# Group norm statistics of a retention head moved from VectorE to ScalarE, and a state waited for by name

## The chip, the cores and the metric

The kernel runs on one core of a Trainium2 chip. The metric is the device time of one execution in microseconds (us). A core has five engines that run side by side, each through its own queue in order: TensorE (PE in the profile; its weight loads are PEld), VectorE (DVE), ScalarE (ACT), GpSimd (POOL) and SyncE (SP), which here issues all DMAs. They wait for each other through semaphores.

## What is computed

Two layers of a mixer over 1024 rows of width 1024, and a final RMSNorm. In each layer the normalised and modulated rows are projected to 4096 columns; half of them feed four retention heads of width 128, half eight stick-breaking heads of width 64; both halves are gated and projected back. The change lies in the retention, at its end:

```python
def retention(q, k, v):
    ...
    o_inner = jnp.einsum('bhncm,bhnme->bhnce', scores, vc)
    ...
    def step(state, kv_i):
        return state * chunk_dec[None, :, None, None] + kv_i, state
    ...
    o_cross = jnp.einsum('bhncd,nbhde->bhnce', qc, prev) * q_dec[None, :, None, :, None]
    o = (o_inner + o_cross).reshape(b, h, s, v.shape[-1])
    mu = jnp.mean(o, axis=-1, keepdims=True)
    var = jnp.mean(jnp.square(o - mu), axis=-1, keepdims=True)
    return (o - mu) * lax.rsqrt(var + EPS)
```

and then `y_ret = merge_heads(y_ret) * jax.nn.silu(rg)`.

## The kernel before

**Work.** Float32 values are split into two float16 parts (high and low), and each product is three float16 matmuls (high by high, high by low, low by high). Weights come as 128x512 pieces (`wst`), are split on ScalarE and VectorE into `w`, and the normalised rows lie transposed in `hh` and `hl`. A layer runs its four pairs of stick-breaking heads (`stick_project`, then `attend`, `head_pair`, `head_block`, `weigh`: tiles `z`, `beta`, `keep`, `ta`, `av`) and its four retention heads (`retention_project`, `retain`) in an order given by a table, and ends with `out_project`.

**A retention block.** A head has 8 blocks of 128 rows, so that there are 64 blocks in two layers. `retention_project` makes 24 matmuls of 128x512 into `acc` (query, key, value, gate), and starts `retain` for the block. That rotates query and key (`t1`, `t2`, VectorE and GpSimd), splits them, transposes them by DMA into `qkT`, makes the key-value product `pkv` for the state (`rst`, its float16 parts `rs16`; not for the last block), the scores (`psc`), masks and splits them, and adds the products of query by old state and of scores by values in `po`. Then come the statistics: BN_STATS and BN_AGGR on VectorE give mean and variance (`rbs`, `rmv`), GpSimd adds the epsilon column (`rve`) and takes the power -1/2 (`rrs`), VectorE makes `y0` = (po - mean) x gate, and ScalarE and VectorE scale `y0` by `rrs` into the two parts of `yt`. Two blocks' `yt` are transposed by one DMA into `y`, which only `out_project` reads. Up to three blocks are under way at once; `po`, `psc`, `z` and others share five PSUM banks.

**What sets the order.** Nobody writes the order of instructions out. Each piece of work is a generator (a stream) that yields what it needs next: tiles, names marked as done, room in a pool. A planner (`Flow`) keeps a clock for each engine, gives every recorded operation a price, and goes on with the stream of the best rank that is ready by its estimate, TensorE's clock leading, with a slack of 400 on streams that come back to TensorE. The order so found is the order of each engine's queue. A changed price therefore moves work everywhere. At the start, the planner also orders the loads, squares and transposes of the input (`xt`), and the column sums of the first layer's modulation (`sums` from the weights `ada`, 16 matmuls of one column a group).

All recorded operations go through one helper, so that the trace shows them all at line 90; they are told apart by their tiles.

Of the kernel before, what the change touches and what calls it, by code (L numbers as in the profile page):

```python
# [13 lines left out]
F32 = mybir.dt.float32  # L14
AF = mybir.ActivationFunctionType
ALU = mybir.AluOpType
PSUM = bass.MemoryType.PSUM
DRAM = bass.MemoryType.DRAM

P = 128  # L20
# [6 lines left out]
EPS = 1e-6  # L27
# [5 lines left out]
DS = 1.0 / WS  # L33
AS = 256.0
VS = 16.0
RS = 2.0 ** -10


def retention_constants():
    f = np.float32  # L40
    lg = np.log1p(-(f(2.0) ** (f(-5.0) - np.arange(4, dtype=f)))).astype(f)
    i = np.arange(P, dtype=f)
    m, c = i[:, None], i[None, :]
    same = (i[:, None] // 64) == (i[None, :] // 64)
    later = (c // 64) > (m // 64)
    mask = np.zeros((P, 4, P), f)
    qdec = np.exp((i[:, None] + f(1.0)) * lg[None, :]).astype(np.float64)
    for h in range(4):
        dec = np.exp((np.abs(c - m) - (c + 1)).astype(np.float64) * lg[h])
        mask[:, h] = np.where(same | later, dec * np.exp((m - 127.0) * lg[h]), 0.0) * RS  # L50
    kdec = np.exp((f(127.0) - i)[:, None] * lg[None, :]).astype(f)
    bdec = [float(np.exp(f(P) * lg[h])) for h in range(4)]


    cols = np.concatenate([kdec * f(DS * VS), EPS * P * (VS * RS / qdec) ** 2], 1).astype(f)
    return mask, cols, bdec


# [9 lines left out]


MASK, COLS, BDEC = retention_constants()  # L70


# [27 lines left out]
class Flow:  # L100
# [32 lines left out]
    def price(self, kind, name, outs, ins):  # L133
        n = outs[0].free_size()
        if kind == "pe":
            if name == "transpose":
                return 109 if ins[0].dtype == F32 else 64
            if ins[0].dtype == F32:
                return 210 if n < 16 else 61 + n * 4 / 2.4
            rows, cols = ins[0].shape[0], outs[0].shape[0]  # L140
            turn = 97 * (self.shape not in (None, (rows, cols)))
            self.shape = rows, cols
            if 64 in (rows, cols):
                return turn + max(1.5 + n / 4.8, 27)
            return turn + max(2.5 + n / 2.4, 56)
        if kind == "act":
            scales = sum(1 for a in ins[1:] if a.free_size() == 1)
            return n / 1.2 + (51 if ins[0].space == PSUM else 93) + 93 * scales
        if kind == "dve":
            n = max([n] + [a.free_size() for a in ins])  # L150
            if name == "tensor_tensor_scan":
                return 68 + 2.083 * n
            if name == "bn_stats":
                return 170 + n / 0.96
            if name == "bn_aggr":
                return 217
            scales = sum(1 for a in ins if a.free_size() == 1)
            return (n + 65) / 0.96 + 62 * scales
        if kind == "pool":
            if name == "memset":  # L160
                return 36 + 0.84 * n
            if name == "tensor_scalar" and n > 1:
                return 200 + 0.9 * n
            if n == 1:
                return 500 if outs[0].tensor.name.startswith(("rrs", "rs", "r_")) else 268
            return 20 + 3.1 * n if n < 512 else 150 + 2.1 * n
        if name == "dma_start_transpose":
            return 225 + 0.88 * n
        size = outs[0].free_nbytes() * outs[0].shape[0]
        run = 4 * outs[0].shape[-1]  # L170
        return size / run * (8 + 0.037 * run) / 16
# [121 lines left out]
def trunk(ctx: ExitStack, tc, x, c, norm_g, w_ada, b_ada, w_in, w_out, final_g,  # L293
          rot, rmask, rcols, out):
    nc = tc.nc
    flow = Flow()
    pe, act, dve, pool, sp = (Engine(flow, k, e) for k, e in (
        ("pe", nc.tensor), ("act", nc.scalar), ("dve", nc.vector), ("pool", nc.gpsimd), ("dma", nc.sync)))
# [3 lines left out]
    wk = Slots(flow, ctx.enter_context(tc.tile_pool(name="wk", bufs=2)), 2)  # L302
# [16 lines left out]
    def bank(name, tag="g", bufs=5):  # L319
        return ps.tile([P, 512], F32, tag=tag, bufs=bufs, name=name)  # L320
# [40 lines left out]
    rcols_sb = const.tile([P, 8], F32, name="rcols_sb")  # L361
# [605 lines left out]
    def retain(l, h, b, acc, state, turn, mask):  # L967
# [3 lines left out]
        gs = wk.tile([P, P], F32, tag="rg", bufs=3, name="rg")  # L971
        act.activation(gs, acc[:, 384:512], AF.Sigmoid, scale=DS)
        kdec = rcols_sb[:, h:h + 1]
# [8 lines left out]
        roomrot.n += 1  # L982
        dve.scalar_tensor_tensor(out=vd[:, 1], in0=acc[:, 256:384], scalar=kdec, in1=vd[:, 0],
                                 op0=ALU.mult, op1=ALU.subtract)
        dve.scalar_tensor_tensor(out=gs, in0=acc[:, 384:512], scalar=DS, in1=gs,
                                 op0=ALU.mult, op1=ALU.mult)
        pool.tensor_tensor(out=t1[:, 0::2], in0=t1[:, 0::2], in1=t2[:, 1::2], op=ALU.subtract)
        pool.tensor_tensor(out=t1[:, 1::2], in0=t1[:, 1::2], in1=t2[:, 0::2], op=ALU.add)
        turned = t1.rearrange("p a f -> p (a f)")
# [11 lines left out]
        def product(o, ah, al, bh, bl, start=True, stop=True):  # L1001
            pe.matmul(o, ah, bh, start=start, stop=False)
            pe.matmul(o, ah, bl, start=False, stop=False)
            pe.matmul(o, al, bh, start=False, stop=stop)

        old, old16 = state[0] or (None, None)
        if b < NT - 1:
            yield [vd, rk], roomg.has(), "pe"
            roomg.n -= 1
            pkv = bank("psc")  # L1010
            product(pkv[:, 0:P], rk[:, 0, P:], rk[:, 1, P:], vd[:, 0], vd[:, 1])
            new = wk.tile([P, P], F32, tag="rst", bufs=3, name="rst")
            yield [pkv]
            if b == 0:
                dve.tensor_copy(new, pkv[:, 0:P])
            else:
                dve.scalar_tensor_tensor(out=new, in0=old, scalar=BDEC[h], in1=pkv[:, 0:P],
                                         op0=ALU.mult, op1=ALU.add)
            roomg.n += 1
            new16 = wk.tile([P, 2, P], F16, tag="rs16", bufs=3, name="rs16")  # L1020
            yield [new]
            act.mul(new16[:, 0], new, RS)
            yield [new16]
            dve.scalar_tensor_tensor(out=new16[:, 1], in0=new, scalar=RS, in1=new16[:, 0],
                                     op0=ALU.mult, op1=ALU.subtract)
            state[0] = new, new16
        yield [("qkT", l, h, b)], roomg.has(), "pe"
        roomg.n -= 1
        psc = bank("psc")
# [12 lines left out]
        po = bank("po")  # L1042
        if b > 0:
            product(po[:, 0:P], qkT[:, 0], qkT[:, 2], old16[:, 0], old16[:, 1], stop=False)
        product(po[:, 0:P], sm16[:, 0], sm16[:, 1], vd[:, 0], vd[:, 1], start=(b == 0))
        yield [po]
        st = wk.tile([P, 6], F32, tag="rbs", name="rbs")
        dve.bn_stats(out=st, in_=po[:, 0:P])
        mv = wk.tile([P, 2], F32, tag="rmv", name="rmv")
        dve.bn_aggr(out=mv, in_=st)  # L1050
        ve = wk.tile([P, 1], F32, tag="rve", name="rve")
        pool.tensor_tensor(out=ve, in0=mv[:, 1:2], in1=rcols_sb[:, 4 + h:5 + h], op=ALU.add)
        rs = wk.tile([P, 1], F32, tag="rrs", name="rrs")
        pool.tensor_tensor(out=rs, in0=ve, in1=nhalf[:, 0:1], op=ALU.pow)
        y0 = sm
        dve.scalar_tensor_tensor(out=y0, in0=po[:, 0:P], scalar=mv[:, 0:1], in1=gs,
                                 op0=ALU.subtract, op1=ALU.mult)
        roomg.n += 1
        if b % 2 == 0:
            yield (), roomy.has()  # L1060
# [9 lines left out]
                                 op0=ALU.mult, op1=ALU.subtract)  # L1070
        flow.mark(("yt", l, h, b))
        roomr.n += 1
        if b % 2:
            yield [("yt", l, h, b - 1), ("yt", l, h, b)], None, None, LOADED
            sp.dma_start_transpose(out=y[:, h, b - 1:b + 1].rearrange("p b a q -> p (b a) q"),
                                   in_=both.rearrange("p b a e -> p (b a e)"))
# [302 lines left out]
```

## Time and profile before

| | us |
|---|---|
| median of 3 runs | 1092.58 |
| lowest run | 1087.74 |
| profiled execution, its time | 1092.43 |
| profiled execution, its span | 1090.0 |
| TensorE matmuls busy | 1053.6 (97%) |
| VectorE busy | 879.2 (81%) |
| ScalarE busy | 550.7 (51%) |
| GpSimd busy | 247.7 (23%) |

The span runs from the first to the last instruction, and the time of an execution is a little longer. Busy shares are averages over the span; the ends of matmuls are modelled, so that a busy TensorE may still wait within a stretch. The views below say what an engine waited for.

### The profile page before, as it was taken

Reading aid. Unit: us, or ns where it says so; the run is one execution under the profiler, and the core shown is the slowest. Engines: PE = TensorE matmul, PEld = TensorE weight load, DVE = VectorE, ACT = ScalarE, POOL = GpSimd, SP = SyncE. Lnnn points to the kernel's source line nnn. Section 1 sums busy time; section 2 is a strip of 40 time slices with the busy share of each in tenths; the row PEclk is TensorE's granted clock in tenths of the full one; section 3 lists DMA queues with packets and bytes.
Section 4 is the critical chain, followed back from the end, with each engine's and each line's share of the span. In section 5 each row is a group of like instructions: output and inputs, shape, how many; then the busy total and the mean of one; then the engine's idle time right before and its main releaser. Section 6 shows DMA issues by size and latency. Waiting matters only on the chain. (4 is left out here: it accounts for less than half of the span.)

```text
span 1090.0 us, 18647 instructions
## 1 busy us (share of the span) xinstructions
PE 1053.6 (97%) x6472; PEld 525.4 (48%) x6472; DVE 879.2 (81%) x1673; ACT 550.7 (51%) x1263; POOL 247.7 (23%) x557
## 2 busy tenths in 40 slices
PE   6989999999999999999899999999999999999996
PEld 5834444444455544544445444444454445545443
DVE  2488998899899968999455788976899789999544
ACT  3566556535454455481444555544645555555112
POOL 2382330133014202320100034000133013343002
PEclk8699999999999999999999999999999999999999
DMA  9915756766686746367581565665735473647664
GB/s 291 241 50 137 157 112 150 181 137 162 156 201 150 155 91 143 69 172 180 171 239 61 120 142 104 138 159 120 158 78 139 85 153 71 150 82 175 198 238 144
DMA packets 343901, 159.61 MB, mean 146 GB/s; under 512 B 228032, under 2 KB 319232, under 8 KB 343808
## 3 DMA queue, kind: packets, MB, share of 16 engines
q1 hardware_dynamic: 343808, 158.44, 60.3%
q8 instruction: 50, 0.82, 0.3%
q14 instruction: 43, 0.35, 0.1%
HBM read 92.32 MB, written 11.53 MB: 95 GB/s over the span
## 5 line engine op out<-in xcount | busy, mean ns | idle before, releaser
L90 PE MATMUL acc<-hh,w 128*128 128x512 f16 x1024 | 323.0, 381 | 0.7 <-DVE q L90 0.6
L90 PE MATMUL acc<-w,hh 128*128 128x512 f16 x1024 | 305.0, 379 | 0.0
L90 PEld LDWEIGHTS <-w 128*128 128x128 f16 x1536 | 145.7, 99 | 179.7 <-issue 21.3
L90 PE MATMUL acc<-hl,w 128*128 128x512 f16 x512 | 195.0, 381 | 0.8 <-DVE hl L90 0.8
L90 PE MATMUL acc<-w,hl 128*128 128x512 f16 x512 | 194.0, 379 | 0.0
L90 POOL TENSOR_TENSOR t<-t,t 128x128 f32<-128x128 f32 (+1 forms) x192 | 130.9, 696 | 232.6 <-DVE t L90 196.4
L90 PE MATMUL acc<-w,y 128*128 128x512 f16 (+1 forms) x792 | 170.8, 374 | 3.3 <-ACT y L90 3.1
L90 PEld LDWEIGHTS <-hh 128*128 128x128 f16 x1024 | 92.3, 98 | 96.8 <-issue 10.8
L90 DVE TENSOR_TENSOR_SCAN keep<-keep,own 128x640 f32<-128x640 f32 (+3 forms) x60 | 114.3, 1911 | 18.8 <-ACT keep L90 18.7
L90 PEld LDWEIGHTS <-y 128*128 128x128 f16 x792 | 76.5, 98 | 91.2 <-ACT y L90 3.6
L90 DVE SCALAR_TENSOR_TENSOR w<-wst,w 128x512 f16<-128x512 f32 x160 | 110.8, 714 | 8.2 <-ACT w L90 7.9
L90 ACT ACTIVATE w<-wst 128x512 f16<-128x512 f32 x160 | 96.5, 635 | 15.2 <-DMA wst<-in_w_in_dram 11.9
L90 ACT CAST t<-t 128x256 f16<-128x256 f32 (+1 forms) x128 | 44.3, 352 | 88.5 <-POOL t L90 53.3
L90 ACT CAST keep<-beta 128x640 f16<-128x640 f32 (+3 forms) x60 | 53.0, 885 | 63.5 <-DVE beta L90 63.2
L90 PEld LDWEIGHTS <-hl 128*128 128x128 f16 x512 | 50.1, 98 | 60.4
L90 ACT ACTIVATE keep<-z 128x512 f32<-128x512 f32 (+3 forms) x120 | 63.7, 531 | 20.6 <-PE z L90 20.1
L90 DVE TENSOR_TENSOR keep<-beta,keep 128x640 f16<-128x640 f32 (+3 forms) x60 | 61.2, 1024 | 7.5 <-ACT keep L90 7.5
L90 PE MATMUL z<-k,q 64*128 64x512 f16 (+3 forms) x576 | 64.6, 328 | 1.3 <-ACT beta L90 0.5
L90 ACT ACTIVATE beta<-z 128x512 f32<-128x512 f32 (+4 forms) x120 | 64.3, 536 | 0.0
L90 DVE SCALAR_TENSOR_TENSOR beta<-beta,keep 128x639 f32<-128x639 f32 (+3 forms) x60 | 62.5, 1047 | 0.0
L90 DVE TENSOR_TENSOR t<-acc,turn 128x256 f32<-128x256 f32 x128 | 47.9, 415 | 17.2 <-ACT vd L90 16.2
L90 DVE TENSOR_TENSOR_SCAN both<-both,own 128x128 f32<-128x128 f32 (+3 forms) x64 | 55.1, 869 | 7.2 <-ACT both L90 7.2
(122 smaller groups left out, 1307.4 us busy)
## 6 DMA issues: line engine op xcount, KB each, us to landing
wst<-in_w_in_dram SPq DMA_DIRECT2D x128, 256.0 KB, 3.5
wst<-in_w_ada_dram SPq DMA_DIRECT2D x64, 256.0 KB, 3.1
ada<-in_w_ada_dram SPq DMA_DIRECT2D x16, 512.0 KB, 6.5
wst<-in_w_out_dram SPq DMA_DIRECT2D x32, 256.0 KB, 3.4
x<-xh SPq DMA_DIRECT2D x24, 256.0 KB, 2.6
xt<-in_x_dram SPq DMA_DIRECT2D x8, 512.0 KB, 5.3
turn<-in_rot_dram SPq DMA_DIRECT2D x64, 64.0 KB, 2.3
xt<-x SPq DMA_DIRECT2D x8, 512.0 KB, 4.4
```

The source lines that it names most:

```text
L90: real(*args, **kw)
```

## The change

The statistics of `po` are taken on ScalarE: an ACTIVATE with Identity and scale -1/128, whose accumulator gives the negative mean `nm` (still in a tile named `rmv`), and an ACTIVATE with Square and `nm` as bias, whose accumulator gives the sum of squared differences `sq` (a tile named `rbs`). Their elementwise outputs go to a part of `turned` that is no longer needed. Since `sq` is a sum and not a mean, the epsilon column carries another factor 128, and the gate a factor of the root of 128. `y0` adds `nm` instead of subtracting the mean. The planner's price of an ACTIVATE that also gives an accumulator rises by 186, also where the kernel already had such ones. A block's generator names the state of the block before and goes on only when it is marked.

```diff
-    cols = np.concatenate([kdec * f(DS * VS), EPS * P * (VS * RS / qdec) ** 2], 1).astype(f)
+    cols = np.concatenate([kdec * f(DS * VS), EPS * P * P * (VS * RS / qdec) ** 2], 1).astype(f)
...
-            return n / 1.2 + (51 if ins[0].space == PSUM else 93) + 93 * scales
+            read = 186 * (len(outs) > 1)
+            return n / 1.2 + (51 if ins[0].space == PSUM else 93) + 93 * scales + read
...
-        dve.scalar_tensor_tensor(out=gs, in0=acc[:, 384:512], scalar=DS, in1=gs,
+        dve.scalar_tensor_tensor(out=gs, in0=acc[:, 384:512], scalar=DS * P ** 0.5, in1=gs,
                                  op0=ALU.mult, op1=ALU.mult)
...
+        if b > 0:
+            yield [("state", l, h, b - 1)]
         old, old16 = state[0] or (None, None)
...
             state[0] = new, new16
+            flow.mark(("state", l, h, b))
...
         yield [po]
-        st = wk.tile([P, 6], F32, tag="rbs", name="rbs")
-        dve.bn_stats(out=st, in_=po[:, 0:P])
-        mv = wk.tile([P, 2], F32, tag="rmv", name="rmv")
-        dve.bn_aggr(out=mv, in_=st)
+
+        junk = turned[:, P:]
+        nm = wk.tile([P, 1], F32, tag="rmv", name="rmv")
+        act.activation(junk, po[:, 0:P], AF.Identity, scale=-1.0 / P, accum_out=nm)
+        yield [nm]
+        sq = wk.tile([P, 1], F32, tag="rbs", name="rbs")
+        act.activation(junk, po[:, 0:P], AF.Square, bias=nm[:, 0:1], accum_out=sq)
+        yield [sq]
         ve = wk.tile([P, 1], F32, tag="rve", name="rve")
-        pool.tensor_tensor(out=ve, in0=mv[:, 1:2], in1=rcols_sb[:, 4 + h:5 + h], op=ALU.add)
+        pool.tensor_tensor(out=ve, in0=sq, in1=rcols_sb[:, 4 + h:5 + h], op=ALU.add)
...
-        dve.scalar_tensor_tensor(out=y0, in0=po[:, 0:P], scalar=mv[:, 0:1], in1=gs,
-                                 op0=ALU.subtract, op1=ALU.mult)
+        dve.scalar_tensor_tensor(out=y0, in0=po[:, 0:P], scalar=nm[:, 0:1], in1=gs,
+                                 op0=ALU.add, op1=ALU.mult)
```

The orders that the planner finds differ nearly everywhere, while the number of matmuls of each kind is the same. Three places follow. In the rows, `t_` with a number is the tile of `t1` or `t2` of one block (`y0` lies in it).

ScalarE, the third block of the first head, from its gate to the scaling of its output; first as it stood before:

```order
L90 ACTIVATE rg<-acc 128x128
L90 ACTIVATE vd<-acc,rcols_sb 128x128
L90 ACTIVATE rs_1435<-rst 128x128
L90 CAST t_1442<-t_1441 128x256
L90 CAST t_1337<-t_1337 128x128
L90 ACTIVATE yt<-t_1235,rrs 128x128
```

and with the change:

```order
L90 ACTIVATE rg<-acc 128x128
L90 ACTIVATE vd<-acc,rcols_sb 128x128
L90 ACTIVATE t_1235,rmv<-po 128x128
L90 ACTIVATE t_1235,rbs<-po,rmv 128x128
L90 ACTIVATE rs_1456<-rst 128x128
L90 CAST keep<-beta 128x5x128
L90 CAST t_1439<-t_1438 128x256
L90 ACTIVATE yt<-t_1235,rrs 128x128
```

The two passes over `po` (`rmv` and `rbs` are their sums) stand between a later block's gate and value rows and the next state's split; in 39 of the 64 blocks they stand side by side, as here, in the others one to three instructions stand between.

VectorE, the fourth block of the first head, around the statistics, before:

```order
L90 SCALAR_TENSOR_TENSOR vd<-acc,rcols_sb,vd 128x128
L90 SCALAR_TENSOR_TENSOR rg<-acc,rg 128x128
L90 BN_STATS rbs<-po 128x6
L90 BN_AGGR rmv<-rbs 128x2
L90 SCALAR_TENSOR_TENSOR t_1337<-po,rmv,rg 128x128
L90 SCALAR_TENSOR_TENSOR rst<-rst,psc 128x128
```

and with the change:

```order
L90 SCALAR_TENSOR_TENSOR vd<-acc,rcols_sb,vd 128x128
L90 SCALAR_TENSOR_TENSOR rg<-acc,rg 128x128
L90 SCALAR_TENSOR_TENSOR rs_1535<-rst,rs_1535 128x128
L90 SCALAR_TENSOR_TENSOR t_1342<-po,rmv,rg 128x128
L90 TENSOR_TENSOR t_1438<-psc,mask 128x128
```

The two statistics instructions are gone, and the gated difference `t_1342<-po,rmv,rg` now reads a sum that ScalarE writes; behind it stands the next block's mask.

TensorE, at the start, where the first projection (`acc`), the column sums and the second 32 transposes of the input (`xt`) alternate; one piece of the difference, with + for the changed kernel:

```order
 L90 LDWEIGHTS w
 L90 MATMUL acc<-hh,w 128x512
+L90 MATMUL xt<-ident,xt 128x128 x32
 L90 MATMUL sums<-c_act,ada 128x1 x16
-L90 MATMUL xt<-ident,xt 128x128 x32
-L90 LDWEIGHTS w
-L90 MATMUL acc<-hh,w 128x512
```

The fourth group of 16 column sums, which stood ahead of the transposes, now stands behind them. (In the trace each of these float32 sums has two records, so that a group of 16 reads x32.)

## Rows read from the trace of the kernel before

**Rows 1.** The page, busy time and share of the span of each engine.
```profile
PE 1053.6 (97%) x6472; PEld 525.4 (48%) x6472; DVE 879.2 (81%) x1673; ACT 550.7 (51%) x1263; POOL 247.7 (23%) x557
```

**Rows 2.** The chain that ended last: start us, us, what.
```profile
1006.91 24.61 PE acc L90 x114
```

**Rows 3.** Waits of TensorE: who waited for whom, us in total, times, longest.
```profile
PE bgp L90 <- DMA rows<-in_norm_g_dram: 8.9, 1, 8.9
PE psc L90 <- DMA rqkT<-t: 4.0, 3, 1.5
PE acc L90 <- ACT y L90: 3.1, 2, 1.6
...
PE psc L90 <- POOL t L90: 1.3, 5, 0.5
...
PE psc L90 <- POOL both L90: 0.2, 1, 0.2
```

**Rows 4.** Busy us by window (PE, PEld, DVE, ACT, POOL); last row: tile rmv, DVE, POOL.
```profile
100.00:200.00 100.00, 99.48 (x607) 46.40 (x606) 94.20 (x186) 56.99 (x136) 23.94 (x55) 1.00 0.70 154
900.00:1000.00 100.00, 99.21 (x690) 50.25 (x690) 91.98 (x225) 55.52 (x147) 40.73 (x83) 1.00 0.50 110
...
900.00:1000.00 100.00, 7.46 (x28) 2.66 (x14) 1.00 0.50 110
```

**Rows 5.** Groups of instructions by form: busy us, mean ns | idle before.
```profile
L90 ACT ACTIVATE vd<-acc,rcols_sb 128x128 f16<-128x128 f32 x64 | 23.4, 366 | 0.0
...
L90 DVE BATCH_NORM_STATS2 rbs<-po 128x6 f32<-128x128 f32 x64 | 18.3, 287 | 3.3 <-PE po L90 3.1
...
L90 ACT ACTIVATE rg<-acc 128x128 f32<-128x128 f32 x64 | 17.6, 275 | 28.6 <-PE acc L90 28.6
...
L90 DVE BATCH_NORM_AGGREGATE rmv<-rbs 128x2 f32<-128x6 f32 x64 | 11.6, 182 | 2.2
...
L90 ACT ACTIVATION_READ_ACCUMULATOR junk<-xt 128x1 f32 x22 | 4.1, 187 | 0.0
```

**Rows 6.** Timeline of ScalarE, a square of the input and its accumulator read: start, us.
```profile
28.10 1.06 ACT L90 ACTIVATE junk<-xt 128x1024 bf16<-128x1024 f32 x1
29.06 0.19 ACT L90 ACTIVATION_READ_ACCUMULATOR junk<-xt 128x1 f32 x1
```

**Rows 7.** Timeline around the first block's statistics.
```profile
118.70 0.27 DVE L90 BATCH_NORM_STATS2 rbs<-po 128x6 f32<-128x128 f32 x1
...
119.22 0.35 DVE L90 SCALAR_TENSOR_TENSOR t<-po,rmv,rg 128x128 f32<-128x128 f32 x1
...
119.27 0.19 POOL L90 TENSOR_TENSOR rve<-rmv,rcols_sb 128x1 f32<-128x1 f32 x1 [2.97 <-DVE rmv L90]
```

**Rows 8.** Waits of all engines: ScalarE's scaling of the output.
```profile
ACT yt L90 <- POOL rrs L90: 16.6, 23, 2.7
```

**Rows 9.** Timeline of TensorE at the start.
```profile
26.93 3.73 PE L90 MATMUL sums<-c_act,ada 128*128 128x1 f32 x32 [0.41 <-DVE sh L90]
...
40.56 6.82 PE L90 MATMUL sums<-c_act,ada 128*128 128x1 f32 x32
47.24 6.10 PE L90 MATMUL xt<-ident,xt 128*128 128x128 f32 x32
...
63.73 0.35 PE L90 MATMUL sums<-ones,acc 128*128 128x1 f32 x2 [0.67 <-DVE acc L90]
...
73.13 0.38 PE L90 MATMUL sums<-ones,ada 128*128 128x1 f32 x2 [1.32 <-POOL ada L90]
...
78.41 0.38 PE L90 MATMUL sums<-ones,ada 128*128 128x1 f32 x2 [1.50 <-POOL ada L90]
```

**Rows 10.** Windows at the start; behind POOL: granted clock, DMA share, GB/s.
```profile
18.10:24.90 6.80, 6.80 (x34) 6.74 (x34) 1.71 (x4) 0.92 (x2) 0.00 (x0) 0.50 0.89 288
...
31.70:35.10 3.40, 3.40 (x12) 1.73 (x9) 1.54 (x4) 3.36 (x4) 2.35 (x4) 0.50 1.16 294
...
38.50:52.20 13.70, 13.70 (x62) 12.50 (x61) 4.03 (x9) 4.83 (x7) 3.79 (x4) 0.50 0.95 241
```

## The prediction

> **What bounds the kernel now.** I began with the page's busy times: TensorE's matmuls cover 1053.6 us of a span of 1090.0, 97% [rows 1]. That row alone proves little, since matmul ends are modelled, so I looked at the pace. In the chain of waits, late in layer 1, 114 output matmuls of 128x512 stand back to back and take 24.61 us [rows 2]: 0.216 us each. In such stretches TensorE does nothing but its next matmul, and only fewer matmuls, a higher clock or less waiting could shorten it. How much waiting there is, the view of waits on TensorE says: 17 rows, from 8.9 us down to 0.2 us, sum 27.1 [rows 3]. The 8.9 us are the wait for the first loads, before any of the changed code, and stay. So 18.2 us, 1.7% of the span, is all that better overlap can return; a loss has no such limit.
>
> Next, how near the other engines are to taking over. In the windows, VectorE is busy 94.2 us of 100 in the fullest stretch of retention and ScalarE never over 57.0 [rows 4]. VectorE is the one close to the edge, but TensorE's list of waits has only small rows that name it.
>
> **The change, part by part.** The sum is made against the profiled execution: span 1090.0 us, time 1092.43, which is 0.15 under the median of the runs shown.
>
> *VectorE.* BN_STATS (287 ns) and BN_AGGR (182 ns) go, 64 of each [rows 5]: 64 x 0.469 = 30.0 us less work. The two pieces of VectorE's order show it: between the gate product and the subtraction nothing of the statistics is left. By the bottleneck this is worth 0. At most it is worth those waits on TensorE that a loaded VectorE causes.
>
> *ScalarE.* Two ACTIVATE and two accumulator reads for each of 64 blocks. Nearest rows: a 128x128 read from PSUM without a pointer operand is 275 ns (rg), with one 366 ns (vd, pointer as scale instead of bias), an accumulator read 187 ns [rows 5]. Upper bound by durations: 0.275 + 0.187 + 0.366 + 0.187 = 1.015 us a block, 65 us. Lower bound: instructions overlap on ScalarE, as the read that starts 0.10 us before the square in front of it ends, at 29.06 against 28.10 + 1.06 [rows 6]; four such overlaps take 0.40 off: 0.615 us a block, 39 us. I take the lower end for load. ScalarE goes from 550.7 to about 590 us (616 at the upper end), 54% to 57%. No second table load is in the order, so Identity and Square cost no switch. The densest window of retention holds 14 blocks, two VectorE rows each, in 900 to 1000 us [rows 4]; at 1.015 us they make its 55.5 into 70: ScalarE is not the bound. Price on the path: 0.
>
> *The chain behind po.* Before, BN_STATS starts at 118.70, the subtraction that frees the bank at 119.22, the add on GpSimd at 119.27: 0.52 and 0.57 us [rows 7]. After: Identity and its read 0.36, about 0.09 for the hand-over, so the subtraction can start at about 0.45; Square 0.366 + 0.09 and a hand-over put the add at about 1.0 us. So the bank is freed as early as before by VectorE, but Square reads it too, until about 0.8. The add comes 0.4 us later, the gated output with it. What hides this: no product waits for a block's output before the output projection, and there the last block's transposed output is first needed after the four products of another half. On ScalarE the output's scaling now waits 16.6 us for GpSimd in 23 places [rows 8]; expect more. Behind it in the queue stand casts of the next blocks, and TensorE would feel those only if they were late by more than the lead that the order gives. That lead: between a block's projection and its score product there are 33 of the 128x512 matmuls in the median before (7.1 us at 0.216), and 33 after; between the score product and po 13.5 before, 12 after. Without this cover, 0.4 us x 64 = 26 us would show.
>
> *The state by name.* The generator of block b goes on to the key-value product when the state of b-1 is marked. Nothing is issued for it. That product needs 3 matmuls, and the state is used only for new = old x decay + product, so I price it at 0; if a product were held back by a whole VectorE and ScalarE round, about 1 us, it would still be inside the lead of 33 matmuls.
>
> *The planner's order.* The price of an accumulated ACTIVATE rises by 186 everywhere, so the order changes from the first microseconds, where Square sums the input rows. The multiset of matmuls is the same, 6380 in both orders, and so are the changes between full-height and 64-row matmuls, 241 and 242. TensorE's bare work is unchanged: 0.
>
> One place is moved in a way that I can price. At the start the second 32 transposes stand ahead of the fourth group of 16 column sums instead of behind it. Before, that group runs 40.56 to 47.38 and takes 6.82 us where an earlier one took 3.73; the transposes come at 47.24 [rows 9]. The granted clock there is 0.50 from 38.5 to 52.2, the 1.2 GHz level; each of three such stretches (18.1, 31.7, 38.5) begins during or just after column sums, and the last ends some 5 us after its sums do [rows 10]. With transposes in between, I expect two shorter stretches of some 5 us each in place of 13.7: (13.7 - 10) / 2 = about 2 us gained. Bounds: 0 to -6.8 if the stretch vanished, +6.8 if as much again ran at half clock. Second, the transposes' copies reach VectorE and GpSimd up to 6.7 us earlier. These two then prepare the later columns, and TensorE waits for them at 63.73, 73.13 and 78.41 by 0.67, 1.32 and 1.50 us [rows 9], 3.5 us. I take half to all of this as gone, some 2 us.
>
> Sum: 1092.4 + 0 (TensorE's work) + 0 (engines off the path) - 2 (clock) - 2 (start waits) = 1088.4 us, or 0.4% less. The other waits of some 14 us, for transposed keys (4.0), for the last y (3.1) and smaller ones [rows 3], I keep at their size: the order moves them about, and the reason of each, a transfer or the drain of a last block, remains.
>
> **Against the change** speaks a rule of the Trainium skill, "ScalarE: Activation LUTs", section "Rules for kernel authors": additions and multiplications belong on VectorE, not ScalarE. The rows here bear out that the statistics cost more where they go: 0.469 us of VectorE against 0.615 to 1.015 of ScalarE. Were the difference on the path, 64 x 0.15 to 0.55 = 9 to 35 us would be added, 1102 to 1128 us. That is worked into rival B.
>
> **Rivals.** *A: the middle gains as well.* VectorE's 30 us shorten the way from projection to score product, and the 5.5 us of waits before psc (4.0, 1.3, 0.2) [rows 3] go, with the small ones behind VectorE, about 8 us in all: 1080. For it: VectorE at 94%. Against: the largest of these waits names a DMA, not VectorE. Chance 0.15.
>
> *B: a wait takes the place of the removed work (the other side).* VectorE's subtraction now waits for ScalarE's mean, in a queue that stands still meanwhile; behind it stand the next block's mask and rotation, on which the score product depends. Where ScalarE is late by one foreign 128x512 activation, 0.6 us, in half the 64 blocks, VectorE loses 19 us, of which 30 us of freed time absorbs all until lateness exceeds 0.47 us a block in the mean. Beyond that it eats the lead; at 0.4 us a block on TensorE it is +26: 1115. A milder form, +8 to +15, gives 1097 to 1104. For it: 39 of 64 pairs of passes stand adjacent on ScalarE, so the second waits for the first one's sum at the head. Against: ScalarE has 43% idle time. Chance 0.17, of which 0.04 for over 1114.
>
> *C: the start gets worse.* The column sums after the transposes pull the clock down for the first projection: up to +6.8, 1099. Chance 0.08.
>
> **How the numbers follow.** The forecast as summed, its own range 1084 to 1094, has 0.60. From 1079, below A's 1080 by a little, to 1100, which takes in C and half of B's milder form, I leave out some 0.05 below and 0.13 above. About 2% is what a measurement of this kernel can tell from no change, here 22 us. Faster by that would need more than all the waits that can move, unless the clock helps too: 0.02. Slower by that needs B in its hard form: 0.05. Within 2%: 0.93.
>
> **What would show it.** Right: VectorE near 849 us, ScalarE 590 to 616, TensorE's busy time within a few us of 1053.6 (it counts slow-clock matmuls at their length), its waits after the first load 14 to 18 us, fewer at 60 to 80 us, and fewer half-clock microseconds before 60. Wrong: rows in TensorE's waits that grow at score, state or po products with VectorE or ScalarE behind them (B), VectorE idle for the mean by more than 20 us in all, or a half-clock stretch over the first projection (C). What would overturn the whole is a wait at the layer boundary or at the end that the new order makes longer, for the lead counts above do not cover the output projection.

## The result, and the profile after

The changed kernel takes 1097.51 us in the median of 6 runs (1094.41 to 1102.27), the kernel before 1089.32 in runs beside them: a ratio of 1.0083, 95% interval 1.0055 to 1.0112. So it is slower by 0.8%, some 9 us, where 0.4% less was forecast. Of the six runs of the kernel before, one of 1222.69 us was slow and is not in the ratio. The time lies outside the forecast's own range (1084 to 1094), inside the wide one (1079 to 1100), and on the wrong side of no change. The profiled execution has a span of 1096.4 us and a time of 1098.16.

The page's busy times, against [rows 1]:

```profile
PE 1051.2 (96%) x6472; PEld 518.8 (47%) x6472; DVE 847.5 (77%) x1545; ACT 590.1 (54%) x1519; POOL 276.3 (25%) x557
```

VectorE and ScalarE came out as forecast (849 and 590). TensorE's busy time is the same within 2.4 us, and the span is 6.4 us longer: TensorE waits more. GpSimd, which the forecast priced at nothing, has the same 557 instructions and 28.6 us more of busy time.

TensorE's waits, with whom it waited for, us in total, times and longest, against [rows 3]; 17 rows, whose sum is 36.4 us against 27.1 (27.3 without the first load, where 14 to 18 were forecast):

```profile
PE bgp L90 <- DMA rows<-in_norm_g_dram: 9.1, 1, 9.1
PE psc L90 <- POOL t L90: 8.8, 11, 2.1
PE acc L90 <- ACT y L90: 3.9, 1, 3.9
...
PE psc L90 <- DMA rqkT<-t: 2.9, 7, 1.3
```

The wait for the rotated tile `t` from GpSimd, 1.3 us before, is 8.8 now. That is most of the 9.3 us. The bank's name misleads here: `psc` is the name of two products, the key-value product, which reads `t` itself (`psc<-vd,t`), and the score product, which reads `t` as the DMA has transposed it (`psc<-rqkT`). By form, all 8.8 us stand before the key-value product:

```profile
L90 PE MATMUL psc<-vd,t 128*128 128x128 f16 x168 | 20.9, 221 | 9.7 <-POOL t L90 8.8 <-ACT beta L90 0.8
```

The wait for the last output `y` is one of 3.9 us where there were two with 1.6 as the longest.

Two windows, against [rows 4] (busy us of PE, PEld, DVE, ACT and POOL, then granted clock), and the end of the chain, against [rows 2]:

```profile
100.00:200.00 100.00, 96.64 (x593) 45.48 (x594) 88.57 (x164) 58.48 (x162) 26.83 (x56) 1.00 0.69 153
900.00:1000.00 100.00, 95.94 (x648) 47.58 (x644) 81.06 (x178) 59.12 (x190) 48.12 (x77) 1.00 0.50 104
```
```profile
1028.86 22.78 PE acc L90 x105
```

In both retention stretches VectorE is freer (94.20 to 88.57, 91.98 to 81.06) and TensorE is less busy (99.48 to 96.64, 99.21 to 95.94) at full clock. GpSimd has grown. In the chain the output matmuls run at 0.217 us, as before (0.216).

The groups by form show which instructions of GpSimd grew. First the kernel before, a row that was not read ahead of the prediction, then the changed one; then VectorE's subtraction and ScalarE's scaling in the changed kernel (busy us, mean ns | idle before):

```profile
L90 POOL TENSOR_TENSOR rrs<-rve,nhalf 128x1 f32<-128x1 f32 x64 | 41.7, 652 | 5.0
```
```profile
L90 POOL TENSOR_TENSOR rrs<-rve,nhalf 128x1 f32<-128x1 f32 x64 | 56.9, 889 | 5.0
L90 POOL TENSOR_TENSOR rve<-rbs,rcols_sb 128x1 f32<-128x1 f32 x64 | 29.1, 454 | 92.1 <-ACT t L90 92.1
L90 ACT ACTIVATE yt<-t,rrs 128x128 f16<-128x128 f32 x64 | 25.8, 404 | 36.6 <-POOL rrs L90 25.1 <-POOL beta L90 5.6 <-POOL both L90 3.5
L90 DVE SCALAR_TENSOR_TENSOR t<-po,rmv,rg 128x128 f32<-128x128 f32 x64 | 21.7, 340 | 2.4 <-ACT t L90 2.3
```

The power went from 652 to 889 ns and the epsilon add, 0.19 us in [rows 7], to 454, although each handles 128 numbers as before. ScalarE's scaling waits 25.1 us for the power (16.6 in [rows 8]). VectorE stands idle ahead of the subtraction for only 2.4 us in all, which speaks against rival B as it was put.

A timeline shows one such place:

```profile
951.37 2.32 POOL L90 TENSOR_TENSOR t<-t,t 128x128 f32<-128x128 f32 x2 [3.50 <-DVE t L90]
...
953.50 1.80 DVE L90 TENSOR_TENSOR_SCAN keep<-keep,own 128x768 f32<-128x768 f32 x1
...
953.65 1.64 POOL L90 TENSOR_TENSOR rve<-rbs,rcols_sb 128x1 f32<-128x1 f32 x1
...
955.37 0.55 POOL L90 TENSOR_TENSOR rrs<-rve,nhalf 128x1 f32<-128x1 f32 x1
955.88 0.67 POOL L90 TENSOR_TENSOR t<-t,t 128x256 f16<-128x256 f32 x1
...
956.61 0.23 PE L90 MATMUL psc<-vd,t 128*128 128x128 f16 x1 [2.06 <-POOL t L90]
```

The add starts 0.15 us after a VectorE scan of stick-breaking and ends with it, at 955.29 against 955.30: 1.64 us for 128 additions. Behind the add and the power in GpSimd's queue stands the low part of the next block's `t`, whose high part ScalarE had cast by 954.13, and behind that tile waits TensorE, 2.06 us. The statistics' small operations are not needed soon, but they stand in the queue in front of something that is.

Not every wait for `t` is of this kind. From 940 to 1010 us the view of waits has four:

```profile
PE psc L90 <- POOL t L90: 4.0, 4, 2.1
```

In each of these the timeline has the add and the power straight ahead of the low part of `t`. In the other seven, 4.7 us, neither stands there: GpSimd has rotated the block and idles some 0.5 us until ScalarE has cast the high part. What makes those late was not tested.

The layer boundary has another place, on ScalarE and TensorE:

```profile
527.41 1.06 ACT L90 ACTIVATE junk<-xt 128x1024 bf16<-128x1024 f32 x1 [1.76 <-DMA xt<-x]
...
529.50 1.15 ACT L90 ACTIVATE xt<-xt,rs 128x1024 f32<-128x1024 f32 x1 [0.94 <-POOL rs L90]
530.55 0.60 ACT L90 CAST y<-y 128x512 f16<-128x512 f32 x1
...
531.21 1.03 PE L90 MATMUL acc<-w,y 128*128 128x512 f16 x2 [3.86 <-ACT y L90]
```

VectorE begins the last `y` at 527.40 and takes 0.69 us, but its cast stands in ScalarE's queue behind the square and the scaling of a residual row, the first of which waits for its load and the second for GpSimd. TensorE stands for 3.86 us and then runs at half clock (granted 0.50 from 531.2 to 534.0 us). Just ahead of that it waits twice for a transfer, 2.03 and 0.64 us, where the kernel before has one such wait of 0.5:

```profile
PE av L90 <- DMA ta<-keep: 2.7, 2, 2.0
```

Windows 510 to 550 us, before and after, with the granted clock as the third number from the end:

```profile
510.00:550.00 40.00, 36.50 (x216) 19.02 (x215) 25.60 (x33) 15.80 (x22) 2.95 (x8) 1.00 0.67 185
```
```profile
510.00:550.00 40.00, 33.47 (x191) 17.11 (x189) 17.75 (x26) 14.46 (x20) 2.95 (x8) 0.91 0.62 147
```

At the start, the same columns for 17 to 53 us, before and after:

```profile
17.00:53.00 36.00, 35.59 (x202) 31.71 (x202) 13.64 (x31) 15.86 (x24) 9.83 (x16) 0.67 0.99 268
```
```profile
17.00:53.00 36.00, 35.11 (x221) 26.18 (x221) 21.04 (x46) 23.73 (x45) 14.33 (x23) 0.81 1.02 283
```

The clock is higher there, as forecast. By the instant at which TensorE has done the same bare work, the changed execution is 5.8 us ahead at 54 us.

### The profile page after: what moved, and what is told of

Same layout as the page of the kernel before. It is cut to its first block, busy times and chain, and to the rows that moved or that the text cites. A ratio compares the mean times of both kernels' runs of the same rounds, so it can differ in the third digit from the quotient of the medians.

```text
span 1096.4 us, 18803 instructions
## 1 busy us (share of the span) xinstructions
PE 1051.2 (96%) x6472; PEld 518.8 (47%) x6472; DVE 847.5 (77%) x1545; ACT 590.1 (54%) x1519; POOL 276.3 (25%) x557
## 4 chain that ended last, share of the span: by engine, by line
PE 47%; DVE 11%; issue 6%; POOL 4%; DMA 4%; ACT 4%; SPq 2%; POOLq 0%; DVEq 0%; ACTq 0%
PE acc L90 40%; PE z L90 3%; POOL t L90 2%; PE av L90 2%; DVE t L90 2%; DMA rqkT<-t 2%; SPq L90 2%; DMA ta<-keep 1%; DVE keep L90 1%; POOL rrs L90 1%; PE psc L90 1%; DVE home L90 1%; PE po L90 1%; DVE beta L90 1%; DVE w L90 1%
## 5 line engine op out<-in xcount | busy, mean ns | idle before, releaser
L90 POOL TENSOR_TENSOR t<-t,t 128x128 f32<-128x128 f32 (+1 forms) x192 | 128.0, 680 | 257.2 <-DVE t L90 223.2
L90 DVE SCALAR_TENSOR_TENSOR w<-wst,w 128x512 f16<-128x512 f32 x160 | 110.7, 713 | 14.4 <-ACT w L90 13.9
L90 ACT CAST t<-t 128x128 f16<-128x128 f32 (+1 forms) x128 | 42.9, 353 | 77.6 <-DVE t L90 45.3
L90 POOL TENSOR_TENSOR rrs<-rve,nhalf 128x1 f32<-128x1 f32 x64 | 56.9, 889 | 5.0
```

The costliest lines, as they stand in the source:

```text
L90: real(*args, **kw)
```

## The experiments

Ratios are to the kernel before, with 95% intervals. To take an order and a computation apart, an instruction was moved or replaced while the planner was told the old one (`flow.note`; `.real` issues past the planner), so that the queues of TensorE and SyncE keep their order to the word. The state waited for by name, alone, leaves all five engines' orders of the kernel before word for word as they are, so there was nothing to run: its price of 0 held there.

In the expectations, C is the theory that GpSimd's add and power fall beside VectorE's operations and hold up the rotation behind them, O that the planner's new order alone costs the time, and H that VectorE waits for ScalarE's sums.

**e1 and e2: the order and the statistics apart.** e1 has the changed kernel's order, with the statistics back on VectorE:

```diff
...
-        act.activation(junk, po[:, 0:P], AF.Identity, scale=-1.0 / P, accum_out=nm)
...
+        dve.real.bn_stats(out=st6, in_=po[:, 0:P])
+        dve.real.bn_aggr(out=mv, in_=st6)
+        flow.note("act", "activation", [junk, nm], [po[:, 0:P], nm])
...
```

> The order of the changed kernel on all engines, with BN_STATS and BN_AGGR of VectorE back at the place where the first pass stood. Theory C (collision): the longer way of the statistics puts GpSimd's two small operations (rve, rrs) beside VectorE's long two-input operations, which stretch them, and the next block's rotation waits behind them. Then here rrs goes back to about 0.65 us in the mean (0.889 in the changed kernel, 0.652 before), TensorE's waits for the rotation (psc on GpSimd's t) fall from 8.8 us to under 4, and the time is 1088 to 1092 us. Theory O (order): the loss is the planner's new order alone; then nothing of this moves and the time stays at 1095 to 1099 us. The start's gain of some 7 us and the wait of 3.9 us for y at the layer boundary stay under both.

Measured: 1.0107 (1.0081 to 1.0133), a median of 1102.85 us: slower than the changed kernel, and outside the ranges of both theories. TensorE's waits, and GpSimd's add and power:

```profile
PE psc L90 <- POOL t L90: 6.0, 8, 1.5
PE po L90 <- DVE t L90: 3.8, 10, 0.9
```
```profile
L90 POOL TENSOR_TENSOR rrs<-rve,nhalf 128x1 f32<-128x1 f32 x64 | 49.8, 778 | 5.0
L1064 POOL TENSOR_TENSOR rve<-rmv,rcols_sb 128x1 f32<-128x1 f32 x64 | 28.4, 443 | 92.2 <-DVE rmv L1057 92.0
```

C wanted the power back at 0.65 us and the waits under 4; they are 0.778 and 6.0. The long add (0.443) is there without ScalarE's passes.

e2 is the reverse, the kernel before with the two passes on ScalarE noted as BN_STATS and BN_AGGR.

> The order of the kernel before on all engines, with the two passes on ScalarE in place of BN_STATS and BN_AGGR, one behind the other at their place. Theory C: rrs grows beyond 0.8 us in the mean, the waits of psc for the rotation grow from 1.3 us to 6 or more, 1094 to 1100 us. Theory O: within 2 us of the kernel before, 1088 to 1091 us. Theory H (head of line): VectorE's subtraction waits for ScalarE's mean, seen as idle time of VectorE before it of 10 us or more.

Measured: 1.0047 (1.0020 to 1.0075). The time is in C's range, but C's signs are not there (the power 0.732 us, the wait for `t` 2.9 us); H's is: VectorE idles 27.0 us before the subtraction. So the order is the larger part: it costs 1.07% by itself, though it was planned for statistics on ScalarE, and within it the move of the statistics even returns 0.24% (1.0107 to 1.0083), with intervals that overlap. In the old order the move costs about half a per cent.

**e3: the price alone.** The kernel before with the two lines of the planner's price.

```diff
-            return n / 1.2 + (51 if ins[0].space == PSUM else 93) + 93 * scales
+            read = 186 * (len(outs) > 1)
+            return n / 1.2 + (51 if ins[0].space == PSUM else 93) + 93 * scales + read
```

> The kernel before with the planner's price of an accumulated ACTIVATE raised by 186, nothing else. Its order is that of the changed kernel up to the first retention blocks. All theories: the start gains some 7 us at 80 us, as in the changed kernel. Theory C: statistics stay on VectorE, so little of it is given back in the middle and the time is 1080 to 1085 us. Theory O: a new order gives it back, 1089 to 1097 us. If the layer boundary's wait for y belongs to the price it shows here as 3 to 5 us.

Measured: 1.0031 (1.0010 to 1.0053), as O had it; C's gain did not come. The start is that of the changed kernel, and it is lost again, in part at a place of its own, the end of the first layer's heads (columns as in the windows above):

```profile
460.00:480.00 20.00, 13.66 (x94) 6.17 (x92) 15.83 (x37) 12.40 (x32) 5.17 (x17) 0.86 0.78 172
```

TensorE is busy 13.66 of 20 us there (17.76 in the kernel before). The boundary's wait for `y` was 1.3 us, so that wait does not come from the price alone.

**e4 and e5: without add and power.** The epsilon add and the power are left out and the output is scaled by a constant, so that the normalisation is not computed; e4 in the changed kernel, e5 in the one before.

```diff
-        pool.tensor_tensor(out=ve, in0=sq, in1=rcols_sb[:, 4 + h:5 + h], op=ALU.add)
-        pool.tensor_tensor(out=rs, in0=ve, in1=nhalf[:, 0:1], op=ALU.pow)
+        flow.note("pool", "tensor_tensor", [ve], [sq, rcols_sb[:, 4 + h:5 + h]])
+        flow.note("pool", "tensor_tensor", [rs], [ve, nhalf[:, 0:1]])
...
```

> The changed kernel in its own order with GpSimd's epsilon add and power left out: the gated output is scaled by a constant instead, so its output is another one. Theory C with the queue as the way: GpSimd has the rotation alone, the waits of psc for it fall from 8.8 us to about 2, and the time to 1088 to 1092 us. If the rotation itself is stretched, and not delayed by what stands ahead of it, the waits stay at 6 us or more and the time at 1094 to 1098 us. Theory O: 1095 to 1099 us.

> The kernel before in its own order, with GpSimd's epsilon add and power left out as in e4_new_no_power (a constant scales the gated output, so the output is another one). This gives what the two operations cost where VectorE makes the statistics. Theory C (they collide and delay the rotation only where ScalarE makes the statistics late): a gain of under 4 us, 1086 to 1092 us beside a kernel before of 1089 to 1092. Theory G (they cost the same in either kernel, and e4's gain of 12 us over the changed kernel says nothing of the change): a gain of 9 us or more.

Measured: e4 0.9974 (0.9953 to 0.9995), e5 0.9987 (0.9959 to 1.0015). The two small operations cost 0.0109 of the time in the changed kernel, 12 us, and some 1.4 us in the one before, 4.5 at most. In e4 the wait for GpSimd shrinks from 8.8 us to

```profile
PE psc L90 <- POOL t L90: 2.5, 5, 0.8
```

Not all of the 12 us need be that wait. In e4's profiled execution the boundary too costs 4 us less, though its wait for `y` is still 3.2 us: the two waits for a transfer ahead of it, 2.7 us, are gone, and the half clock behind it was shorter (0.96 granted from 510 to 550 us). Nor does e4 tell GpSimd's queue from ScalarE's: without the power, ScalarE's scaling no longer waits for it (25.1 us in the changed kernel).

**e6 and e7: only the add moved,** to ScalarE in the changed kernel, to VectorE in the one before.

```diff
-        pool.tensor_tensor(out=ve, in0=sq, in1=rcols_sb[:, 4 + h:5 + h], op=ALU.add)
+        act.real.activation(ve, sq, AF.Identity, bias=rcols_sb[:, 4 + h:5 + h])
+        flow.note("pool", "tensor_tensor", [ve], [sq, rcols_sb[:, 4 + h:5 + h]])
```

> The changed kernel in its own order, with the epsilon add as an Identity with bias on ScalarE behind the second pass; GpSimd keeps the power alone. Theory C: about a third to a half of what e4 gained comes back, 4 to 6 us against the changed kernel, ratio to before 1.002 to 1.005, waits of psc for the rotation 4 to 6 us. If ScalarE's queue is what hurts, 64 more instructions of 0.3 us make it slower than the changed kernel, over 1.0083.

> The kernel before in its own order, with the epsilon add on VectorE behind BN_AGGR. GpSimd's queue is shorter by 0.19 us a block, VectorE's longer by some 0.15 us. Theory C: the power starts at the same time as before and collides as little, within 2 us of the kernel before. It would be a faster version only if GpSimd's queue costs in the kernel before as well (theory G), then 2 to 4 us faster.

Measured: e6 1.0023 (1.0000 to 1.0046), e7 0.9995 (0.9968 to 1.0022). One add less on GpSimd gives back 6.5 us of 9 in the changed kernel, nothing in the one before. In the profile of e6 the wait for `t` is 5.3 us, 3.5 less, and ScalarE's wait for the power 14.4, 10.7 less.

**e8 and e9: the cast.** The one cast of `y` at the layer boundary goes from ScalarE to VectorE; e9 has this and e6's add.

```diff
-                act.copy(hi, parts)
+                if (l, p, ch) == (0, 3, 1):
+                    dve.real.tensor_copy(hi, parts)
+                    flow.note("act", "copy", [hi], [parts])
+                else:
+                    act.copy(hi, parts)
```

> The changed kernel in its own order, with one instruction moved: the cast of the last pair's y of layer 0 from ScalarE, where it stands behind a square of a residual row that waits for its load, to VectorE. TensorE's wait for this y (3.9 us at 527) should fall to about 1.5 us, as before, and the time by 2 to 3 us if the layer boundary is on the path; the clock's dip at 529 to 536 may go with it, another 1 to 3 us. If the stall only moves to the next load, the time stays.

> The changed kernel in its own order with both edits of e6 and e8: the epsilon add on ScalarE, the one cast of y on VectorE. If GpSimd's queue and the layer boundary are two causes of their own, the gains add: 1.0083 - 0.0060 - 0.0045 gives 0.998, or 2 us faster than the kernel before. If both are the same loss seen twice, the ratio stays at 1.002 to 1.004.

Measured: e8 1.0038 (1.0013 to 1.0062), e9 0.9990 (0.9966 to 1.0014). In e8 the wait and the window at the boundary are

```profile
PE acc L90 <- DVE y L936: 1.3, 1, 1.3
```
```profile
510.00:550.00 40.00, 35.91 (x215) 19.06 (x214) 22.06 (x32) 17.05 (x25) 3.48 (x8) 1.00 0.69 189
```

with no half clock left. The intervals of e8 and of the changed kernel just overlap. 1.0083 - 0.0060 - 0.0045 = 0.9978 was to come from both, and 0.9990 did. Two edits bring the changed kernel back to the time of the one before, not past it. The wait for `t` is still 6.3 us in e9's profile, so that row alone does not measure what GpSimd's operations cost.

**e10: the stretching by itself.** Behind the kernel's own work, GpSimd makes four pairs of a 128x1 power and a 128x1 add while VectorE repeats one 128x512 operation.

> The kernel before, and behind its end six stretches in which GpSimd does four powers and four adds of 128x1: alone, and beside VectorE operations of 128x512 of five kinds: a copy, a subtraction and a scalar_tensor_tensor of two SBUF tensors, a scan of two, and a scalar_tensor_tensor of one PSUM and one SBUF tensor. Theory C: power and add keep 0.55 and 0.19 us alone, beside the copy and beside the one that reads PSUM, and stretch to two times or more beside the three with two SBUF inputs. If they keep their lengths everywhere, what stretches them in the kernel is something else.

Measured, timeline at the end (start, us): alone; beside a copy; a difference of two SBUF tensors; a scan; a product that reads PSUM and SBUF. L1391 is the power, L1392 the add:

```profile
1085.07 0.55 POOL L1391 TENSOR_TENSOR ur<-ones,nhalf 128x1 f32<-128x1 f32 x1
1085.58 0.19 POOL L1392 TENSOR_TENSOR uq<-ones,nhalf 128x1 f32<-128x1 f32 x1
...
1086.38 6.43 DVE L1368 COPY uo<-ua 128x512 f32<-128x512 f32 x14
...
1087.31 0.45 POOL L1392 TENSOR_TENSOR uq<-ones,nhalf 128x1 f32<-128x1 f32 x1
...
1092.84 10.15 DVE L1371 TENSOR_TENSOR uo<-ua,ub 128x512 f32<-128x512 f32 x14
...
1094.05 0.26 POOL L1392 TENSOR_TENSOR uq<-ones,nhalf 128x1 f32<-128x1 f32 x1
...
1113.21 11.29 DVE L1378 TENSOR_TENSOR_SCAN uo<-ua,own 128x512 f32<-128x512 f32 x9
...
1114.38 0.54 POOL L1391 TENSOR_TENSOR ur<-ones,nhalf 128x1 f32<-128x1 f32 x1
1114.89 0.79 POOL L1392 TENSOR_TENSOR uq<-ones,nhalf 128x1 f32<-128x1 f32 x1
1115.63 0.54 POOL L1391 TENSOR_TENSOR ur<-ones,nhalf 128x1 f32<-128x1 f32 x1
...
1124.61 10.12 DVE L1382 SCALAR_TENSOR_TENSOR uo<-pu,ub 128x512 f32<-128x512 f32 x14
...
1125.28 0.19 POOL L1392 TENSOR_TENSOR uq<-ones,nhalf 128x1 f32<-128x1 f32 x1
```

Beside the scan a pair takes 1115.63 - 1114.38 = 1.25 us, one scan (11.29 / 9). Beside the difference the add takes 0.26, and a pair one difference (10.15 / 14 = 0.73) where it takes 0.65 alone; beside a product of two SBUF tensors, the fifth kind, it is the same. So GpSimd goes on where one of VectorE's instructions ends. Beside the product that reads PSUM, as long as the difference, it runs as if alone. A miss: the plain copy stretches the add too (0.45), and the power keeps its 0.54 us, which fits that the add in front of it does the waiting. The Trainium skill has a rule for such pairs in "SBUF — State Buffer", section "Who interferes with whom": a VectorE instruction with two SBUF inputs keeps out a GpSimd instruction that reads SBUF, and one with at most one such input does not, outside modes that a copy can enter. The probe agrees on the rows with two SBUF inputs and on the one that reads PSUM; that the copy was in such a mode no row shows. I had not weighed that section in the forecast.

**e11: e2 with the add on ScalarE,** e6's edit in the old order.

> e2_old_order_new_stats with the epsilon add on ScalarE as in e6. Theory C: half or more of e2's loss of 0.47% goes, ratio 1.000 to 1.003. If e2's loss comes from VectorE waiting for the mean or from ScalarE's load, the ratio stays at 1.004 or rises.

Measured: 1.0053 (1.0029 to 1.0077), a miss for C: in the old order the add was not what e2 lost by. **e12 to e14** take that up. e12 puts e2's two sums in tiles of their own, as the changed kernel has them:

```diff
-        act.real.activation(junk, po[:, 0:P], AF.Square, bias=mv[:, 0:1], accum_out=mv[:, 1:2])
+        act.real.activation(junk, po[:, 0:P], AF.Square, bias=mv[:, 0:1], accum_out=st[:, 0:1])
```

> The order of the kernel before, statistics on ScalarE, as in e2, but the two sums in two tiles, as the changed kernel has them. In e2 both sums lay in one tile, and VectorE's subtraction waited for the Square there and not only for the mean: its row 'DVE t <- ACT t' is 26.4 us in 28 places, against 7.1 in 12 in the changed kernel. Theory H (e2's 0.47% is VectorE waiting for ScalarE): most of the row goes, under 8 us, and the ratio falls to 0.999 to 1.002. Theory C (GpSimd's two small operations come later and fall beside VectorE's): they come as late as in e2, so the ratio stays at 1.003 to 1.006.

Measured: 1.0037 (1.0012 to 1.0063), and VectorE's wait did not go; L1051 is the Square:

```profile
DVE t L90 <- ACT t L1051: 26.2, 28, 2.9
```

So the sums' tile was not what it waited for. e13 keeps the statistics on VectorE and adds the two passes as work that nobody reads:

```diff
         dve.bn_aggr(out=mv, in_=st)
+        more = wk.pool.tile([P, 2], F32, tag="more", bufs=2, name="more")
+        junk = turned[:, P:]
+        act.real.activation(junk, po[:, 0:P], AF.Identity, scale=-1.0 / P, accum_out=more[:, 0:1])
+        act.real.activation(junk, po[:, 0:P], AF.Square, bias=more[:, 0:1], accum_out=more[:, 1:2])
```

> The kernel before with the two passes added on ScalarE as extra work whose sums nobody reads; VectorE keeps BN_STATS and BN_AGGR and its own mean, and GpSimd's add starts as early as before. Theory L (ScalarE's 40 us of load and the bank held longer cost the time): 1.003 to 1.006, as e2. Theories H and C: no one waits for ScalarE's sums, so 0.999 to 1.001.

Measured: 1.0370 (1.0332 to 1.0408), far from every expectation. The timeline around one block, and the waits:

```profile
118.71 0.27 DVE L90 BATCH_NORM_STATS2 rbs<-po 128x6 f32<-128x128 f32 x1
...
119.08 0.28 ACT L1053 ACTIVATE t<-po 128x128 f32<-128x128 f32 x1 [1.31 <-DVE rbs L90]
...
119.74 0.19 ACT L1054 ACTIVATION_READ_ACCUMULATOR t<-po,more 128x1 f32 x1
...
119.97 0.35 DVE L90 SCALAR_TENSOR_TENSOR t<-po,rmv,rg 128x128 f32<-128x128 f32 x1 [0.77 <-ACT t L1054]
```
```profile
ACT t L1053 <- DVE rbs L90: 109.0, 56, 4.7
DVE t L90 <- ACT t L1054: 52.2, 64, 2.6
```

The subtraction uses VectorE's own mean. What it has in common with the two passes is the bank of `po`, which all three only read, and the tile `turned`, into one half of which the passes write and into the other the subtraction. It starts 0.04 us after the second pass has ended (the row counts such a wait in each of the 64 blocks). The first pass waits for BN_STATS in the same way, and these two share the bank alone. That halves of one tile do not by themselves keep two engines apart, the start of the kernel before shows, where both copy into parts of `xT` at once:

```profile
25.25 0.69 DVE L90 COPY xT<-xt 128x512 f32<-128x512 f32 x1 [0.84 <-PE xt L90]
25.68 0.59 ACT L90 COPY xT<-xt 128x512 f32<-128x512 f32 x1 [0.52 <-PE xt L90]
```

So readers of one bank on two engines take turns in this program. VectorE stands for 52.2 us, ScalarE for 109.0, and the kernel is 40 us slower; which of the two stands costs how much of it was not separated. The Trainium skill has this in "PSUM — Partial Sum Buffer", section "PSUM bank collisions raise a hardware error": instructions of different engines on one bank and the same partitions are to be kept apart by a dependency, two reads as well. The waits in the trace fit that dependency.

e14 is e12 without add and power (the normalisation is not computed there either).

> As e12, with the epsilon add and the power on GpSimd left out and the output scaled by a constant (so the normalisation is not computed). Theory C: what e12 shows over 0.999 goes, as e4 took 0.0109 off the changed kernel: 0.997 to 1.000. Theory H: nothing in VectorE's wait for the mean changes, so it stays within 0.002 of e12.

Measured: 1.0007 (0.9982 to 1.0032). 0.0030 goes although VectorE's wait for the Square, 29.9 us, does not. That speaks for C, but it is no clear verdict: 1.0007 lies between the ranges of C and H, and the intervals of e12 and e14 overlap. How e2's and e12's 0.4% divides between the two causes stays open.

## Why the prediction was wrong

**Right.** VectorE's 30 us (31.7) and ScalarE's 39 us (39.4); TensorE's bare work; the state by name, 0; and that VectorE's load is not what bounds (0.24% came back for 30 us).

**The step that failed first is "the chain behind po … what hides this".** I asked who waits for the block's output and found nobody before the output projection. That holds, and the path still had a price: the add and the power stand in GpSimd's queue ahead of the next block's rotated key, on which the key-value product depends. I gave them no price wherever the order put them. They took 0.454 and 0.889 us in the mean, 0.50 a block more than before (0.190 + 0.652), 32 us of GpSimd; TensorE's wait for `t` grew by 7.5 us, and taking both operations out returns 12. The lead of 33 matmuls, which I had taken for cover, was counted to the wrong product. Between a block's projection and its key-value product, which waits for `t` first, the same count in the trace gives 21 of the 128x512 matmuls in the median, 4.5 us at 0.216, in both kernels; the 11 products that waited had 6 to 27. What sets the durations is where the operations fall beside VectorE's work: with BN_STATS on VectorE, e1 has nearly the same (0.443 and 0.778) and a wait of 6.0 us, so it is the order more than the later sums. That the operations cost these 12 us is shown by e4 and e5; the way from them to TensorE is shown for four waits, 4.0 us, and stays open for the rest.

**The second is "the other waits … I keep at their size".** The wait for the last `y` at the layer boundary had a reason that remains, but its length is set by what the order puts ahead of one cast on ScalarE. It went from 1.6 to 3.9 us, with a half-clock stretch behind it; e8, which moves that cast alone, prices both at 0.0045, 4.9 us. The prediction's last sentence had named this place, and the sum had no term for it.

**The start was about right, and in part by luck.** Forecast -4 us, half for the clock and half for the waits at 63, 73 and 78 us. Those waits went from 3.5 to 1.7 us, as forecast. For the clock, the two profiled executions differ by 5.8 us at 54 us, but that is not the order alone. In 9 profiled executions with the old order there, the clock of 17 to 53 us was 0.67 in six, 0.76 in e12 and 0.86 in e10 and e14:

```profile
17.00:53.00 36.00, 35.59 (x233) 27.95 (x233) 18.55 (x41) 21.86 (x38) 14.54 (x21) 0.86 1.06 284
```

In 7 with the new order it was 0.73 to 0.81. By the instant of equal work at 54 us, the means are 4.7 and 1.6 us ahead of the profile of before: some 3 us for the order. One execution against one could have shown anything from a gain of 7 us to a loss of 4.

**Rival B had a true part and named the wrong reason.** The subtraction waits not for the mean but for the Square's read, 0.89 us after the first pass starts in e13's timeline, where I had put it at 0.45. In the changed kernel's order other work fills that time, 2.4 us of idleness in all; in the old order it is 26 us, which eats what the removed statistics freed. e13, where VectorE keeps its statistics, stands 52 us there and is 40 slower. Rival A's gain in the middle and rival C's worse start did not come.

**An account,** from runs of different pairs and not a proof: start -3, GpSimd +10.5 (e4 less e5), boundary +4.9, freed VectorE -2.6 (e1 to the changed kernel), together +9.8 us, against 9.0 measured. The closeness proves little: each of the last three terms has an interval of some 4 us to either side, and e4's gain holds part of the boundary's, so that the terms count something twice.

## What to carry to other kernels

Cover is a property of a queue, not of a result: for every moved instruction, ask what stands behind it on its engine and who waits for that, even when its own output is needed by nobody soon. Tiny GpSimd operations on SBUF are not tiny beside long VectorE operations with two SBUF inputs, and in this program two engines that read one PSUM bank take turns, so splitting a tile's readers between engines has a price. A cover counted in matmuls is to be counted to the product that reads the tile first. Where a planner reorders everything, keep its order while exchanging one computation, and the computation while exchanging the order: here that showed the order to be the larger term.

## What was not expected of the hardware

A 128x1 add on GpSimd took 0.19 us alone and beside VectorE products with one operand in PSUM, 0.79 beside 128x512 scans, and 1.64 once beside a 128x768 scan in the changed kernel. The same instructions at the start got a granted clock of 0.67, 0.76 or 0.86 over 36 us, from one execution to the next.
